# A stick-breaking attention trunk on one core: the hold on the next weights moved from ScalarE's tile to GpSimd's, and one block of w per head pair multiplied by VectorE

## The chip, the core and the metric

The kernel runs on one core of a Trainium2 chip. The core has TensorE (PE in the profile; PEld is its weight load), VectorE (DVE), ScalarE (ACT), GpSimd (POOL) and SyncE (SP), which here issues all the DMA transfers of the program's own. The five engines run their own instruction streams, each in the order in which the program was built, and meet through semaphores. The metric is the device time of one execution in microseconds (us); a kernel's time is the median over its runs.

## The reference, cut to what matters

One layer: half a SwiGLU block, stick-breaking attention, half a SwiGLU block, each behind an RMS norm, on 1024 rows of 1024 columns. The change touches the attention alone (16 heads of 64):

```python
qkv = xn @ w_qkv                       # q, k normalised per head
z = q . k / sqrt(64)                   # per head, blocks of 128 queries
A[t,s] = sigmoid(z[t,s]) * prod_{s<j<t} (1 - sigmoid(z[t,j]))   # s < t
o = A @ v ;  x = x + o @ w_o
```

## The kernel before, in words

Every matrix product is made of three passes: an operand is split into a high part (a copy in fp32r, made by ScalarE) and a low part (the rest, a subtraction made by GpSimd or VectorE), and high x high, low x high and high x low are summed in PSUM. The rows are stored in reverse order, so that the product over j becomes a scan that runs forward.

The attention works on eight **pairs of heads**, one after the other. While the scores of pair p are worked on, TensorE also computes q, k and v of pair p+1 ("fills", `qkv`, nine or six matmuls at a time, 128x384, on the banks bq), and the weights of pair p+2 are loaded and split (`weights_of`). A pair has four parts a to d (head 1 or 0, rows of the lower or upper half).

- **Scores** (`scores`): for each block `(tb, kb)` TensorE writes z into a bank bz (L817), ScalarE makes two sigmoids of it (L821: into w, and in place in bz), VectorE runs the product scan over bz into the tile om (L823), and GpSimd multiplies w by om (L830), after a memset of one column (L828) where a row block begins. For the upper half of the rows om lies in the same buffer as w and the profile calls both w.
- **Values** (`values`): TensorE transposes w by blocks into a bank bt (L852), ScalarE copies that into th (L179), VectorE subtracts th from the bank into tl (L180), and TensorE multiplies th and tl with v into the bank bo (L870). There are two tiles each of th and tl and two banks bt.
- **Weights of pair p+2** (`weights_of`): four steps k = 0, 2, 4, 6 per pair. A step loads `raw_qkv` by two DMAs (L701; 192 KB each), makes the high part wqh of it (L707, ScalarE, 128x768) and the low part wql (L710, GpSimd, two of 128x384). Steps 0 and 2 fill one pair of tiles wqh and wql, steps 4 and 6 another; I call them the **first tile** and the **second tile**. `raw_qkv` has two buffers, so the load of a step can begin only when the copy and both subtractions of the step two before it are done.
- **The hold**: without more, the copy could run as soon as its load has landed. Before L707 a step therefore lets GpSimd write a value that is thrown away, made from a place of qk that is computed late in pair p+1's fills (L706): into one column of wqh. ScalarE's copy overwrites that column and so has to wait for GpSimd's write.
- **Order**: the code gives every piece of work a place in time (`PARTS`, `FILLS`, `LOADS`, in us of a plan), sorts by it, and the framework's scheduler then settles when the program is built in which order each engine issues its instructions. Nothing is reordered on the chip: an instruction that waits holds up all that stand behind it on its engine.

The names in the profile: q_s, kh_s, kl_s are the splits of q and k (L779 on ScalarE, L780 on VectorE) from banks bz that hold transposed qk (L775); sq, qk and vst (L739, L740, L743) are ScalarE's three readings of a finished fill; o (L875, L876) is a finished output, which is split into w tiles (L179, L180) and stored (o_keep).

Of the kernel before, what the change touches and what calls it, by code (L numbers as in the profile page):

```python
# [13 lines left out]
ALU = mybir.AluOpType  # L14
# [3 lines left out]
P = 128  # L18
# [85 lines left out]
def macaron_kernel(ctx, tc, x, g1, w1_in, w1_out, gm, w_qkv, gq, gk, w_o, g2, w2_in, w2_out, out):  # L104
    nc = tc.nc
    act, dve, pool_e, pe, sp = nc.scalar, nc.vector, nc.gpsimd, nc.tensor, nc.sync
# [42 lines left out]
    def bank(tag):  # L149
        p, used = psum[-1]  # L150
        if tag not in IN_TURN:
            return p.tile([P, NHALF], F32, name=tag, bufs=BANKS[tag])
        i = used[tag] = (used.get(tag, -1) + 1) % BANKS[tag]
        return p.tile([P, NHALF], F32, name=f"{tag}{i}", bufs=1)
# [434 lines left out]
    with pools(*RAWS) as pr:  # L589
# [41 lines left out]
        with banks("ps2"), pools(*SECOND) as pl:  # L631
            lay_banks()
            gain_m = load_gain(pn, gm)
            half = pn["xs"].tile([P, 4, 2], F32, name="half", bufs=1)
# [41 lines left out]
    with ExitStack() as stack:  # L676
# [9 lines left out]
        def weights_of(p, state, behind=None):  # L686

            wh, wl = state["wq"] = {}, {}

            def step(n, k):
                if k % 4 == 0:
                    wq = pl[f"wq{(2 * p + k // 4) % 4}"]
                    state["h"], state["l"] = (wq.tile([P, 4, 3 * P], F32R, name=f"wq{n}", bufs=1) for n in "hl")
                h_, l_ = state["h"], state["l"]
                raw = pl["raw_qkv"].tile([P, 2, 3, P], F32, name="raw_qkv")
                src = w_qkv[k * P : (k + 2) * P, :].rearrange("(k p) (a c) -> p k a c", p=P, a=3)
                for i in range(2):  # L700
                    sp.dma_start(raw[:, i], src[:, i, :, p * P : (p + 1) * P])  # L701
                ks = slice(k % 4, k % 4 + 2)
                raw = raw.rearrange("p k a c -> p k (a c)")
                if behind:
                    there = behind[n]()
                    pool_e.tensor_tensor(h_[:, k % 4, 0:1], there, there, op=ALU.mult)  # L706
                act.activation(h_[:, ks], raw, AF.Copy)  # L707
                for i in range(2):
                    k_ = k % 4 + i
                    pool_e.tensor_tensor(l_[:, k_, :], raw[:, i, :], h_[:, k_, :].bitcast(F32), op=ALU.subtract)  # L710
                    wh[k + i], wl[k + i] = h_[:, k % 4 + i, :], l_[:, k % 4 + i, :]

            return [partial(step, i // 2, k) for i, k in enumerate((4, 6, 0, 2) if p == 0 else (0, 2, 4, 6))]
# [83 lines left out]
        def scores(state, hd, half):  # L797

            w = state["w", hd, half] = {}

            def step(tb, kb):
                L = T - tb * P
                if kb == half:
                    t = pl["w"].tile([P, T - tb % 4 * P], F32, name=f"w{hd}{tb % 4}", bufs=1)

                    om = t[:, L : 2 * L] if half else pl["om"].tile([P, T], F32, name="om")
                    state["om"], w[tb] = om, t[:, :L]
                om, wt = state["om"], w[tb]
                q = state["q", hd, half][:, (tb % 4) * P : (tb % 4 + 1) * P]
                s0 = max(tb * P, kb * NHALF)  # L810
                n = (kb + 1) * NHALF - s0
                c0 = s0 - tb * P
                off = P if n == P else 0
                z = bank("bz")
                keys = slice(s0 - off - kb * NHALF, NHALF)
                for i in range(2):
                    pe.matmul(z[:, : off + n], q, state["k", hd, kb][i][:, keys], start=i == 0, stop=i == 1)  # L817

                z = z[:, off : off + n]
                for to, sign in ((wt[:, c0 : c0 + n], 0), (z, 1)):  # L820
                    act.activation(to, z, AF.Sigmoid, scale=state["f", half][:, sign, tb % 4, hd : hd + 1])  # L821
                least = first[:, P : P + 1].to_broadcast([P, n]) if c0 else first[:, :n]
                dve.tensor_tensor_scan(  # L823
                    om[:, c0 : c0 + n], z, least, initial=om[:, c0 - 1 : c0] if c0 else 0.0,
                    op0=ALU.mult, op1=ALU.max,
                )
                if c0 == 0:
                    pool_e.memset(wt[:, 0:1], 0.0)  # L828
                c1 = max(c0, 1)
                pool_e.tensor_tensor(wt[:, c1 : c0 + n], wt[:, c1 : c0 + n], om[:, c1 - 1 : c0 + n - 1], op=ALU.mult)  # L830

            return [partial(step, tb, kb) for tb in range(half * 4, half * 4 + 4) for kb in range(half, 2)]

        def values(state, p, hd, half):
# [263 lines left out]
```

## Time and profile before

| What | us |
|---|---|
| Time before, median of 3 runs (lowest, highest) | 1968.99 (1968.15, 1970.13) |
| The profiled execution's own time | 1967.96 |
| Its span in the trace | 1966.2 |
| One steady pair, from one transpose L852 to the same one of the next pair (814.91 to 881.74) | 66.83 |
| TensorE busy in that pair | 64.89 |
| VectorE, ScalarE, GpSimd busy in that pair | 52.29, 51.29, 38.34 |

The trace has the eight pairs between some 700 us and 1240 us from the span's start; feed-forward blocks lie before and behind. Five steady pairs follow each other at the same distance, so a place in one pair is found again 66.8 us later. In a line of the timeline the first number is the start in us, the second the duration, then engine, line, operation, tiles and shapes; square brackets give how long the engine sat idle just before, and which instruction ended that idle time.

### The profile page before, as it was taken

Reading aid. Unit: us, or ns where it says so; the run is one execution under the profiler, and the core shown is the slowest. Engines: PE = TensorE matmul, PEld = TensorE weight load, DVE = VectorE, ACT = ScalarE, POOL = GpSimd, SP = SyncE. Lnnn points to the kernel's source line nnn. Section 1 sums busy time; section 2 is a strip of 40 time slices with the busy share of each in tenths; the row PEclk is TensorE's granted clock in tenths of the full one; section 3 lists DMA queues with packets and bytes.
Section 4 is the critical chain, followed back from the end, with each engine's and each line's share of the span. In section 5 each row is a group of like instructions: output and inputs, shape, how many; then the busy total and the mean of one; then the engine's idle time right before and its main releaser. Section 6 shows DMA issues by size and latency. Waiting matters only on the chain.

```text
span 1966.2 us, 27322 instructions
## 1 busy us (share of the span) xinstructions
PE 1917.2 (98%) x9656; PEld 1641.7 (83%) x9656; DVE 1248.8 (64%) x1823; ACT 983.4 (50%) x1802; POOL 1086.9 (55%) x957
## 2 busy tenths in 40 slices
PE   7999999999999899999999999999999999999999
PEld 7978888888888798898889897789888888888887
DVE  7855545536767667877787778474645644547644
ACT  6533433443335467777777776344343343343332
POOL 3667666656445445555655645113666666755454
PEclk9999999999999999999999999999999999999999
DMA  5223323238996311111111234411332332359984
GB/s 209 86 93 122 106 88 120 95 123 287 355 321 222 105 33 44 38 39 44 36 37 42 66 103 164 166 60 54 118 102 100 121 102 86 124 195 350 317 274 148
DMA packets 168504, 260.25 MB, mean 132 GB/s; under 512 B 11568, under 2 KB 81200, under 8 KB 168368
## 3 DMA queue, kind: packets, MB, share of 16 engines
q1 hardware_dynamic: 168368, 258.52, 38.3%
q8 instruction: 75, 1.23, 0.3%
q14 instruction: 61, 0.50, 0.1%
HBM read 198.18 MB, written 60.29 MB: 131 GB/s over the span
## 4 chain that ended last, share of the span: by engine, by line
PE 79%; DVE 9%; POOL 4%; ACT 4%; issue 3%; DMA 1%; SPq 0%; ACTq 0%; DVEq 0%; POOLq 0%
PE ka L271 6%; PE ka L272 6%; PE ka L273 6%; PE kc L273 4%; PE kc L272 4%; PE kc L271 4%; PE kb L272 4%; PE kb L273 4%; PE kb L271 4%; PE bq L271 3%; PE bq L272 3%; PE bq L273 3%; PE ma L271 3%; PE ma L272 3%; PE ma L273 3%
## 5 line engine op out<-in xcount | busy, mean ns | idle before, releaser
L180 POOL TENSOR_TENSOR rp<-raw,rp 128x1024 fp32r<-128x1024 f32 x84 | 205.8, 2453 | 189.7 <-ACT rp L179 174.5
L180 POOL TENSOR_TENSOR u<-sf,u 128x512 fp32r<-128x512 f32 x160 | 225.9, 1413 | 152.3 <-ACT u L179 148.4
L180 POOL TENSOR_TENSOR u<-raw,u 128x512 fp32r<-128x512 f32 x136 | 195.8, 1445 | 173.4 <-ACT u L179 172.4
L830 POOL TENSOR_TENSOR w<-w,om 128x512 f32<-128x512 f32 (+4 forms) x128 | 142.4, 1115 | 120.0 <-DVE om L823 93.6
L179 ACT ACTIVATE u<-sf 128x512 fp32r<-128x512 f32 x160 | 100.7, 630 | 215.3 <-PE kb L272 86.8
L390 DVE TENSOR_TENSOR h<-h 128x512 f32<-128x512 f32 x110 | 135.3, 1235 | 88.6 <-POOL h L494 87.9
L271 PE MATMUL bq<-wqh,xh 128*128 128x384 f32 x512 | 174.6, 341 | 2.1 <-DVE vst L744 2.1
L179 ACT ACTIVATE rp<-rh 128x1024 fp32r<-128x1024 f32 (+1 forms) x78 | 76.5, 984 | 198.4 <-issue 65.4
L273 PE MATMUL bq<-wqh,xl 128*128 128x384 f32 x512 | 172.2, 336 | 0.0
L272 PE MATMUL bq<-wql,xh 128*128 128x384 f32 x512 | 172.1, 336 | 0.0
L271 PE MATMUL ka<-xh,u 128*128 128x512 f32 (+1 forms) x448 | 162.2, 362 | 1.9 <-ACT s L442 1.4
L179 ACT ACTIVATE u<-raw 128x512 fp32r<-128x512 f32 x136 | 85.0, 632 | 154.9 <-PE ka L272 101.3
L272 PE MATMUL ka<-xl,u 128*128 128x512 f32 (+1 forms) x448 | 161.9, 361 | 0.0
L273 PE MATMUL ka<-xh,u 128*128 128x512 f32 (+1 forms) x448 | 161.6, 361 | 0.0
L515 DVE TENSOR_TENSOR raw<-raw 128x1024 f32<-128x1024 f32 (+1 forms) x60 | 86.4, 1445 | 96.4 <-DMA raw<-w_out 76.4
L273 PE MATMUL ma<-rp 128*128 128x512 f32 x352 | 137.6, 391 | 3.6 <-DVE rp L180 3.6
L271 PE MATMUL ma<-rp 128*128 128x512 f32 x352 | 137.9, 392 | 0.1
L272 PE MATMUL ma<-rp 128*128 128x512 f32 x352 | 137.6, 391 | 0.0
L821 ACT ACTIVATE w<-bz,f 128x512 f32<-128x512 f32 (+1 forms) x192 | 112.8, 587 | 46.2 <-PE bz L817 40.6
L494 POOL TENSOR_TENSOR h<-h,g 128x512 f32<-128x512 f32 x80 | 112.5, 1406 | 32.7 <-DVE h L446 32.7
L419 DVE TENSOR_TENSOR sf<-raw 128x512 f32<-128x512 f32 x80 | 80.2, 1003 | 78.0 <-POOL u L180 78.0
L180 DVE TENSOR_TENSOR rp<-rh,rp 128x1024 fp32r<-128x1024 f32 (+1 forms) x70 | 110.0, 1590 | 19.2 <-ACT rp L179 16.7
(253 smaller groups left out, 5550.1 us busy)
## 6 DMA issues: line engine op xcount, KB each, us to landing
raw<-w_out SPq DMA_DIRECT2D x120, 512.0 KB, 5.7
raw<-w_in SPq DMA_DIRECT2D x88, 512.0 KB, 3.5
k<-h SPq DMA_DIRECT2D x154, 256.0 KB, 2.1
rh<-k SPq DMA_DIRECT2D x64, 512.0 KB, 6.0
raw_qkv<-w_qkv SPq DMA_DIRECT2D x64, 192.0 KB, 2.9
x_keep<-x SPq DMA_DIRECT2D x32, 256.0 KB, 2.9
x<-x_keep SPq DMA_DIRECT2D x32, 256.0 KB, 5.0
raw<-w_out SPq DMA_DIRECT2D x24, 256.0 KB, 4.2
```

The costliest lines, as they stand in the source:

```text
L179: act.activation(hi, raw, AF.Copy)
L180: (engine or dve).tensor_tensor(lo, raw, hi.bitcast(F32), op=ALU.subtract)
L271: pe.matmul(dst, ah, bh, start=start and i == 0, stop=False, skip_group_check=onto)
L272: pe.matmul(dst, ah, bl, start=False, stop=False, skip_group_check=onto)
L273: pe.matmul(dst, al, bh, start=False, stop=stop and i == n - 1, skip_group_check=onto)
L390: dve.tensor_tensor(src, hb[of[0]], hb[of[1]], op=getattr(ALU, of[2]))
L419: dve.tensor_tensor(f[n], x, y, op=op)
L494: pool_e.tensor_tensor(h, h, gs[k], op=ALU.mult)
L515: dve.tensor_tensor(w[0], w[0], w[1], op=getattr(ALU, W_OF[m][2]))
L821: act.activation(to, z, AF.Sigmoid, scale=state["f", half][:, sign, tb % 4, hd : hd + 1])
L830: pool_e.tensor_tensor(wt[:, c1 : c0 + n], wt[:, c1 : c0 + n], om[:, c1 - 1 : c0 + n - 1], op=ALU.mult)
```

## The change

Two edits. The value that GpSimd writes to hold a step is now written into wql, the low part, in the first column of both row groups that the step fills (two elements), so that only GpSimd's own subtractions come after it; ScalarE's copy no longer has anything of the hold to wait for. And of head 0, lower rows, the last block of the last row group (`tb` 3, `kb` 1: 128x512) is multiplied by om on VectorE, no longer on GpSimd: one block in each of the eight pairs.

```diff
                 if behind:
-                    there = behind[n]()
-                    pool_e.tensor_tensor(h_[:, k % 4, 0:1], there, there, op=ALU.mult)
+                    there = behind[n]().to_broadcast([P, 2])
+                    pool_e.tensor_tensor(l_[:, ks, 0], there, there, op=ALU.mult)
                 act.activation(h_[:, ks], raw, AF.Copy)
...
                 c1 = max(c0, 1)
-                pool_e.tensor_tensor(wt[:, c1 : c0 + n], wt[:, c1 : c0 + n], om[:, c1 - 1 : c0 + n - 1], op=ALU.mult)
+
+                engine = dve if (hd, half, tb, kb) == (0, 0, 3, 1) else pool_e
+                engine.tensor_tensor(wt[:, c1 : c0 + n], wt[:, c1 : c0 + n], om[:, c1 - 1 : c0 + n - 1], op=ALU.mult)
```

Behind L830 the line numbers of the changed kernel are two higher (L852 is L854). The order of the instructions moves as follows; numbers in names are the program's tile numbers, the same in both kernels. The first place is ScalarE at 889 to 900 us of the trace before, where TensorE has just got past the fills of pair p+1; wqh_8906 is a first tile, wqh_9124 the second tile of the same weights. Before:

```order
L821 ACTIVATE bz_8875<-bz_8875,f0_8367 128x256
L707 ACTIVATE wqh_8906<-raw_qkv_8908 128x768
L739 ACTIVATE sq_8889<-bq_8825 128x256
L740 ACTIVATE qk0_8823<-bq_8825 128x256
L743 ACTIVATE vst_8421<-bq_8825 128x2x64
L179 ACTIVATE th_8902<-bt_8897 128x512
L821 ACTIVATE w12_8873<-bz_8915,f0_8367 128x512
L821 ACTIVATE bz_8915<-bz_8915,f0_8367 128x512
L707 ACTIVATE wqh_8906<-raw_qkv_8943 128x768
L779 ACTIVATE q_s1_8937<-bz_8932,gq_sb_6221 64x512
L179 ACTIVATE th_8956<-bt_8952 128x384
```

And now, on the same engine at the same place:

```order
L179 ACTIVATE th_8902<-bt_8897 128x512
L821 ACTIVATE w12_8873<-bz_8915,f0_8367 128x512
L821 ACTIVATE bz_8915<-bz_8915,f0_8367 128x512
L779 ACTIVATE q_s1_8937<-bz_8932,gq_sb_6221 64x512
L707 ACTIVATE wqh_9124<-raw_qkv_9126 128x768
L179 ACTIVATE th_8956<-bt_8952 128x384
L779 ACTIVATE q_s1_8940<-bz_8932,gq_sb_6221 64x512
L821 ACTIVATE w13_8960<-bz_8962,f0_8367 128x128
L821 ACTIVATE bz_8962<-bz_8962,f0_8367 128x128
L707 ACTIVATE wqh_9124<-raw_qkv_9162 128x768
L779 ACTIVATE kh_s1_8979<-bz_8981,gk_sb_6223 128x512
```

The copies of the first tile are gone from here, and those of the second tile stand here instead, one of them ahead of th_8956. The loads raw_qkv_9126 and raw_qkv_9162 go into the buffers of raw_qkv_8908 and raw_qkv_8943. Their own copies have moved to the second place, ScalarE at 840 to 850 us, about 50 us earlier, where the copies of the second tile of the weights before them (wqh_8281) stood. Before:

```order
L179 ACTIVATE th_8256<-bt_8251 128x512
L707 ACTIVATE wqh_8281<-raw_qkv_8283 128x768
L707 ACTIVATE wqh_8281<-raw_qkv_8319 128x768
L779 ACTIVATE kh_s1_8270<-bz_8272,gk_sb_6223 128x512
L179 ACTIVATE th_8295<-bt_8290 128x512
L821 ACTIVATE w02_8310<-bz_8311,f1_7945 128x256
```

Now:

```order
L179 ACTIVATE th_8256<-bt_8251 128x512
L779 ACTIVATE kh_s1_8270<-bz_8272,gk_sb_6223 128x512
L179 ACTIVATE th_8295<-bt_8290 128x512
L707 ACTIVATE wqh_8906<-raw_qkv_8908 128x768
L707 ACTIVATE wqh_8906<-raw_qkv_8943 128x768
L821 ACTIVATE w02_8310<-bz_8311,f1_7945 128x256
L821 ACTIVATE bz_8311<-bz_8311,f1_7945 128x256
L179 ACTIVATE th_8331<-bt_8326 128x512
```

So at both places the copies are now those of loads that come one tile later. The third place is VectorE at 877 to 884 us, where the multiplication comes in (w03_8693 is the tile, om_8694 its product):

```order
 L823 SCALAR_TENSOR_TENSOR om_8694<-bz_8725,om_8694,first_6511 128x512
 L180 TENSOR_TENSOR w13_8720<-o1_8501,w12_8719 128x512
+L832 TENSOR_TENSOR w03_8693<-w03_8693,om_8694 128x512
 L823 SCALAR_TENSOR_TENSOR om_8733<-bz_8734,first_6511 128x512
 L823 SCALAR_TENSOR_TENSOR om_8733<-bz_8751,om_8733,first_6511 128x512
```

VectorE does it behind the split of o and ahead of the next two scans. On GpSimd the subtractions L710 keep their places but for one block of w or two: those of a second tile now stand directly behind their hold, ahead of the multiplication of 128x383 that they followed. TensorE's order in a pair and SyncE's are as before, but for two matmuls of a fill that now stand among the last four of bo.

## Prediction

> **What bounds the kernel now.** I read the page first (busy shares), then the busy times of one steady pair, then the table of waits, then the timeline of each engine through one pair. The page's first line and the stretch of one steady pair (its length, then busy us and instructions of PE, PEld, DVE, ACT and POOL, the granted clock, and the DMA's share and GB/s):
>
> ```profile
> PE 1917.2 (98%) x9656; PEld 1641.7 (83%) x9656; DVE 1248.8 (64%) x1823; ACT 983.4 (50%) x1802; POOL 1086.9 (55%) x957
> 814.91:881.74 66.83, 64.89 (x388) 59.28 (x389) 52.29 (x100) 51.29 (x114) 38.34 (x58) 1.00 0.13 40
> ACT wqh L707 <- POOL wqh L706: 12.3, 6, 2.1
> ```
>
> TensorE sets the time: in a pair it stands still for 66.83 - 64.89 = 1.94 us. So nothing another engine saves is worth more than that a pair, while what makes TensorE wait longer is open above. The third line (who waited for whom, us in total, times, longest) is the wait that the first edit removes: ScalarE stood 2.06 us at the hold, six times. Here is its place, which I call A: ScalarE, then TensorE.
>
> ```profile
> 892.24 0.85 ACT L707 ACTIVATE wqh<-raw_qkv 128x768 fp32r<-128x768 f32 x1 [2.06 <-POOL wqh L706]
> 895.29 0.88 ACT L707 ACTIVATE wqh<-raw_qkv 128x768 fp32r<-128x768 f32 x1
> 896.02 0.69 ACT L779 ACTIVATE q_s<-bz,gq_sb 64x512 fp32r<-64x512 f32 x1
> 896.59 0.49 ACT L179 ACTIVATE th<-bt 128x384 fp32r<-128x384 f32 x1
> 899.12 0.60 ACT L179 ACTIVATE th<-bt 128x512 fp32r<-128x512 f32 x1
> 893.08 0.60 PE L775 MATMUL bz<-ident,qk 128*128 128x128 f32 x4
> 894.33 0.51 PE L870 MATMUL bo<-th,vst 128*128 128x512 f32 x1 [0.65 <-ACT th L179]
> 895.06 0.50 PE L870 MATMUL bo<-tl,vst 128*128 128x512 f32 x1 [0.22 <-DVE tl L180]
> 897.91 0.42 PE L870 MATMUL bo<-th,vst 128*128 128x384 f32 x1
> 898.17 0.41 PE L870 MATMUL bo<-tl,vst 128*128 128x384 f32 x1
> 900.37 0.28 PE L870 MATMUL bo<-th,vst 128*128 128x256 f32 x1
> ```
>
> ScalarE's 2.06 us at the hold made th late, and TensorE waited 0.65 us for th and 0.22 us for tl: 0.87 us of the pair's 1.94.
>
> **The first edit: what the hold now leaves open.** ScalarE's copy waits for its load instead, and at place A the copies now in the queue are those of the second tile, whose loads go into the buffers of the first. A buffer is free when GpSimd has done both subtractions. GpSimd and SyncE at A:
>
> ```profile
> 892.90 0.73 POOL L830 TENSOR_TENSOR w<-w,om 128x255 f32<-128x255 f32 x1
> 893.59 1.96 POOL L710 TENSOR_TENSOR wql<-raw_qkv,wqh 128x384 fp32r<-128x384 f32 x2
> 895.58 20.25 SPq L701 DMA_DIRECT2D raw_qkv<-w_qkv  x8
> ```
>
> Two subtractions ended at 893.59 + 1.96 = 895.55, and the next load was issued at 895.58: it does wait for them, and SyncE had nothing else to do (its order is unchanged, and behind these loads only the stores of o queue). In the changed order the two stand ahead of that multiplication (0.73 us), so the buffer is free at 894.82 in the same frame. The hold itself cannot release GpSimd sooner: it waits for GpSimd's own work on qk just before.
>
> How long from a free buffer to the copy is measured in the ramp, where ScalarE came to two such copies early (GpSimd's four subtractions, SyncE's loads, ScalarE's copies):
>
> ```profile
> 685.79 4.38 POOL L710 TENSOR_TENSOR wql<-raw_qkv,wqh 128x384 fp32r<-128x384 f32 x4 [0.52 <-ACT wqh L707]
> 688.26 9.87 SPq L701 DMA_DIRECT2D raw_qkv<-w_qkv  x8
> 691.94 0.84 ACT L707 ACTIVATE wqh<-raw_qkv 128x768 fp32r<-128x768 f32 x1 [4.79 <-DMA raw_qkv<-w_qkv]
> 694.01 0.84 ACT L707 ACTIVATE wqh<-raw_qkv 128x768 fp32r<-128x768 f32 x1 [1.22 <-DMA raw_qkv<-w_qkv]
> ```
>
> Issue at 688.26, copy at 691.94: 3.68 us. The last subtraction ended at 685.79 + 4.38 = 690.17, the second copy began at 694.01: 3.84 us. ScalarE waited 4.79 and 1.22 us there. I take 3.7. [...]
>
> At A the first copy so starts at 894.82 + 3.7 = 898.5. ScalarE itself is there early: without the hold and the two old copies it is through q_s by about 894.4, and stands some 4 us. The copy frees ScalarE 0.73 us later (895.29 to 896.02), so the 384-wide th runs from 899.25 to 899.75 and tl is ready at some 900.35. TensorE, which took that th at 897.91 and that tl at 898.17, starts them at 899.8 and 900.4: 2.2 us later than before, although its two old waits are gone. Its next th was wanted 900.37 - 898.17 = 2.2 us after that, at 902.6. But the third and fourth subtractions, now behind the multiplication, end at 894.82 + 0.73 + 1.96 = 897.5, the second copy starts at 901.2, and 0.73 us later kh_s and then th follow (about 0.6 us each), ready at 903.15: 0.55 us late, and tl costs some 0.15 us more. TensorE leaves A **2.9 us** later than before. It happens six times. In the ramp the same edit moves two holds; ScalarE waits for loads there already, and I take nothing (1.2 us either way, the wait at 694.01).
>
> Place B, 50 us earlier in the pair, has the first tile's copies now, and the same chain: hold, subtractions of the second tile, loads, copies. GpSimd, ScalarE, TensorE before:
>
> ```profile
> 840.35 0.35 POOL L706 TENSOR_TENSOR wqh<-qk 128x1 fp32r<-128x1 f32 x2
> 844.20 0.65 ACT L179 ACTIVATE th<-bt 128x512 fp32r<-128x512 f32 x1
> 846.45 0.47 ACT L821 ACTIVATE w<-bz,f 128x256 f32<-128x256 f32 x1 [1.60 <-PE bz L817]
> 847.18 0.60 ACT L179 ACTIVATE th<-bt 128x512 fp32r<-128x512 f32 x1
> 848.47 0.48 PE L870 MATMUL bo<-th,vst 128*128 128x512 f32 x1
> 848.79 0.40 PE L870 MATMUL bo<-tl,vst 128*128 128x512 f32 x1
> ```
>
> The hold ends at 840.70; four subtractions of 0.98 us follow at once and free the buffers at 842.66 and 844.62. The copies so start at 846.36 and 848.3, where ScalarE is ready at 844.8. The sigmoid of 846.45 moves to 849.05 and the th of 847.18 to 849.8, done at 850.4; its tl is done some 0.7 us later. TensorE takes them at 850.4 and 851.2, not at 848.47 and 848.79: **2.4 us**, five times (the last pairs load nothing more).
>
> **The second edit.** VectorE multiplies a block of 128x512, which no row of before shows on it. Nearest rows: its subtraction of two tiles of this size in this stage, 0.70 us, and its sums of two in the feed-forward blocks, 1.235 us. Then the place:
>
> ```profile
> L180 DVE TENSOR_TENSOR w<-o,w 128x512 fp32r<-128x512 f32 x14 | 9.8, 699 | 0.0
> L390 DVE TENSOR_TENSOR h<-h 128x512 f32<-128x512 f32 x110 | 135.3, 1235 | 88.6 <-POOL h L494 87.9
> 880.47 1.21 DVE L823 TENSOR_TENSOR_SCAN om<-bz,first 128x512 f32<-128x512 f32 x1
> 883.50 0.68 DVE L180 TENSOR_TENSOR tl<-bt,th 128x512 fp32r<-128x512 f32 x1
> 881.74 0.76 PE L852 MATMUL bt<-ident,w 128*128 128x128 f32 x5 [0.64 <-POOL w L828]
> 884.32 0.41 PE L870 MATMUL bo<-tl,vst 128*128 128x512 f32 x1
> ```
>
> The first is the same stage and the instruction just before it, so I take 0.70. The block takes the scan's place at 880.47 and is done at 881.17, where TensorE had waited until 881.74: that gives back up to 0.54 us. But VectorE runs without a gap there: the scan starts 0.6 us late, a wait of its own swallows 0.2, and the tl of 883.50 ends at 884.6. TensorE took it at 884.32, with 0.14 us to spare. So the gain is spent 3 us on, and 0.3 us is lost: **+0.3**, eight times; bounds are -0.54 (VectorE's lead holds) and +0.85 (1.235 us).
>
> **What the waits do to the clock.** TensorE's waits grow to 3 us, and the trace has such gaps (three rows of TensorE, then stretches behind them; the third figure from the right is the granted clock):
>
> ```profile
> 650.26 0.50 PE L273 MATMUL ma<-rp 128*128 128x512 f32 x1 [3.65 <-DVE rp L180]
> 1129.94 0.39 PE L817 MATMUL bz<-kh_s,q_s 128*128 128x256 f32 x1 [2.05 <-DVE w L823]
> 1189.62 0.33 PE L852 MATMUL bt<-ident,w 128*128 128x128 f32 x1 [1.84 <-POOL w L828]
> 650.00:660.00 10.00, 9.74 (x36) 7.89 (x37) 1.94 (x3) 3.92 (x6) 8.66 (x7) 0.83 0.30 89
> 1130.00:1132.00 2.00, 2.00 (x12) 1.74 (x12) 1.82 (x4) 1.98 (x6) 1.55 (x4) 1.00 0.68 250
> 1190.00:1200.00 10.00, 10.00 (x52) 8.29 (x51) 8.06 (x18) 5.93 (x12) 5.11 (x8) 0.83 0.80 263
> ```
>
> Behind 3.65 us, and behind 1.84 us, ten us ran at 0.83: 1.7 us lost. Behind 2.05 us the clock stayed. A's gap is 3.0 us: without its old waits TensorE is there at 897.91 - 0.87 - 2 x 0.1 (restarts, 0.51 and 0.50 against 0.40) = 896.8, and th comes at 899.8. So I count a dip each time, at 1.0 us net, since a slower TensorE no longer waits the 0.55 + 0.15 us at the second copy: 6 x 1.0 = 6.0. B's gaps are 1.9 and 0.5 us: a dip every other time, 2.5 x 1.7 = 4.2.
>
> **The sum**, in us: A 6 x 2.9 = 17.4; B 5 x 2.4 = 12.0; VectorE's block 8 x 0.3 = 2.4; clock 6.0 + 4.2 = 10.2; less 2.0 for small waits of TensorE as the 0.22 above, which behind 11 longer ones no longer arise (0.2 each). That is +40.0 on the profiled execution's 1967.96 (span 1966.2), so 2008.0; the median lies 1.03 above that execution: **2009.0**.
>
> **Rivals.**
>
> *The loads come in time (faster).* Then the hold was all that kept ScalarE: 6 x 0.87 = 5.2 us are won at A, and 8 x 0.64 = 5.1 at VectorE's block if its lead holds: 1958.7. For it speak the 12.3 us in the waits. Against it: TensorE wants the 384-wide th at 896.8, so the copy would have to start 0.73 + 0.49 us sooner, by 895.6, which is 0.8 us after the buffer is free; two rows say 3.68 and 3.84. Chance 0.07.
>
> *The waits fall into slack.* If th and tl were ahead of TensorE by as much as the copies are late, gains and losses would cancel near 1969. But TensorE already waits for them at A. Chance 0.05.
>
> *No dips.* The clock stays at 1.00, as behind 2.05 us: 40.0 - 10.2 = +29.8, so 1998.8. [...] The trace speaks against it with the dip behind 1.84 us, and for it with the 2.05. Chance 0.22.
>
> *A dip behind every wait of A and B.* Clock 6.0 + 5 x 1.7 = 14.5: 2013.3. Chance 0.16.
>
> **How the numbers follow.** The forecast itself has 0.50. A measurement of this kernel tells about 0.2% (4 us) from no change. All but the first two rivals are slower by more than that: 0.88; faster 0.07; within 0.2% 0.05. Low end of the range: no dips, VectorE's block at -0.54 (8 x 0.84 = 6.7 less), the loads 0.3 us quicker at the eleven places (3.3): 1998.8 - 10.0 = 1988.8, taken as 1988. High end: all dips and the block at 0.85 (8 x 0.55 = 4.4): 2017.7, taken as 2018. Outside lie the two rivals of 0.12 and a little of the rest.
>
> **What would show it.** Right: ScalarE's waits for the hold are gone from the table, and in their place stand waits of L707 for the load of raw_qkv of 3 to 4 us at A and of 1 to 2 us at B, eleven places in all; TensorE's idle time before bo (L872) at the 384-wide th grows from nothing to about 3 us; a steady pair takes 72 to 74 us; the granted clock in a pair falls under 1.00. Wrong in its main step, if L707 waits for no load in the steady pairs; wrong in the second edit, if a pair's wait at the transposes of w is gone and no wait for tl stands 3 us behind it; wrong in the clock, if pairs with 3 us gaps show 1.00.

## The result, and the profile after

The changed kernel takes **2012.95 us** (median of 4 runs, 2011.69 to 2018.98); the kernel before, run beside it, 1969.26 (4 runs, 1968.15 to 1970.13). The ratio is 1.0224, 95% interval 1.0207 to 1.0242: slower, by 43.7 us, where 2009.0 was forecast (1988 to 2018).

The page's first line of the changed kernel, beside the first one shown of before:

```profile
PE 1938.0 (96%) x9656; PEld 1660.0 (82%) x9656; DVE 1259.4 (62%) x1831; ACT 988.5 (49%) x1802; POOL 1078.4 (53%) x949
```

TensorE runs the same 9656 instructions and is busy 20.8 us longer with them, so part of the loss is a slower TensorE; the rest is standing still. A stretch in which the clock is granted at half I call a **dip** (0.50 from 789.00 to 792.41 us, for one). Stretches of the changed kernel, from the 384-wide th of place A to the same one of the next pair, then pieces behind A and B (length, busy us of PE, PEld, DVE, ACT and POOL, granted clock, DMA share, GB/s):

```profile
766.56:842.02 75.46, 68.42 (x389) 62.28 (x389) 52.80 (x102) 52.14 (x113) 36.82 (x57) 0.95 0.12 36
917.80:991.58 73.78, 66.88 (x389) 60.66 (x389) 52.79 (x102) 52.11 (x113) 36.82 (x57) 0.97 0.12 38
766.00:768.00 2.00, 1.29 (x6) 0.81 (x6) 1.31 (x2) 1.95 (x6) 0.10 (x1) 1.00 0.53 155
768.00:772.00 4.00, 3.88 (x15) 3.75 (x15) 2.95 (x5) 3.62 (x8) 0.46 (x1) 0.57 0.00 0
772.00:776.00 4.00, 4.00 (x26) 3.88 (x26) 1.98 (x5) 1.83 (x3) 1.39 (x2) 1.00 0.00 0
788.00:792.00 4.00, 3.68 (x12) 3.12 (x13) 2.85 (x9) 2.48 (x8) 1.28 (x3) 0.63 0.00 0
```

A pair was 66.83 us with TensorE idle for 1.94 of them. The first pair here is 75.46 with 75.46 - 68.42 = 7.04 idle and 68.42 - 64.89 = 3.5 us more busy at a clock of 0.95: two dips, one behind each place. The third pair shows one dip only and is 73.78. Who waited for whom, attention stage (us in total, times, longest):

```profile
ACT wqh L707 <- DMA raw_qkv<-w_qkv: 37.1, 15, 4.4
PE bo L872 <- ACT th L179: 27.6, 11, 3.4
PE bo L872 <- DVE tl L180: 8.9, 17, 0.9
PE bt L854 <- POOL w L828: 1.8, 1, 1.8
```

The row of before in which L707 waits for GpSimd's hold is gone. In its place L707 waits for its load, and TensorE waits eleven times for th. The place itself, in the timeline of the changed kernel: GpSimd and SyncE at A, ScalarE and TensorE at A, then at B, then VectorE's block and the tl behind it, and a row near the end of the program:

```profile
835.89 1.01 POOL L710 TENSOR_TENSOR wql<-raw_qkv,wqh 128x384 fp32r<-128x384 f32 x1
836.92 3.82 SPq L701 DMA_DIRECT2D raw_qkv<-w_qkv  x4
835.74 0.68 ACT L779 ACTIVATE q_s<-bz,gq_sb 64x512 fp32r<-64x512 f32 x1 [0.77 <-PE bz L775]
840.74 0.84 ACT L707 ACTIVATE wqh<-raw_qkv 128x768 fp32r<-128x768 f32 x1 [4.32 <-DMA raw_qkv<-w_qkv]
841.49 0.47 ACT L179 ACTIVATE th<-bt 128x384 fp32r<-128x384 f32 x1
842.02 0.45 PE L872 MATMUL bo<-th,vst 128*128 128x384 f32 x1 [3.27 <-ACT th L179]
843.21 0.84 ACT L707 ACTIVATE wqh<-raw_qkv 128x768 fp32r<-128x768 f32 x1
783.68 0.85 ACT L707 ACTIVATE wqh<-raw_qkv 128x768 fp32r<-128x768 f32 x1 [1.41 <-DMA raw_qkv<-w_qkv]
785.91 0.84 ACT L707 ACTIVATE wqh<-raw_qkv 128x768 fp32r<-128x768 f32 x1 [1.39 <-DMA raw_qkv<-w_qkv]
788.02 0.49 PE L872 MATMUL bo<-th,vst 128*128 128x512 f32 x1 [1.82 <-ACT th L179]
788.81 0.65 PE L872 MATMUL bo<-tl,vst 128*128 128x512 f32 x1 [0.30 <-DVE tl L180]
821.88 0.69 DVE L832 TENSOR_TENSOR w<-w,om 128x512 f32<-128x512 f32 x1
826.25 0.50 PE L872 MATMUL bo<-tl,vst 128*128 128x512 f32 x1 [0.88 <-DVE tl L180]
1992.97 0.50 PE L273 MATMUL ma<-rp 128*128 128x512 f32 x1 [3.57 <-DVE rp L180]
```

Read A from the top: the second subtraction ends at 836.90, the load is issued at 836.92, the copy can begin at 840.74. ScalarE had been free since 836.42 and stood 4.32 us; th, next in its queue, follows at 841.49; TensorE, which had been waiting for it, starts at 842.02 after 3.27 us. The second copy (843.21) waits for nothing. At B both copies wait 1.4 us, and TensorE 1.82 and 0.30.

The last row lies in the feed-forward block, where the change touches nothing. Such a wait, of 3.3 to 3.6 us, stands there in three of the ten profiled executions of this study: with both edits, with the second alone, and with neither (the run below with no hold on GpSimd). This execution took 2018.98, 6 us over the median, and the wait makes most of that. The pairs are not affected.

### The profile page after: what moved, and what is told of

The parts are those of the page before. It is cut to its first block, busy times and chain, and to the rows that moved or that the text cites. A ratio compares the mean times of both kernels' runs of the same rounds, so it can differ in the third digit from the quotient of the medians.

```text
span 2017.2 us, 27373 instructions
## 1 busy us (share of the span) xinstructions
PE 1938.0 (96%) x9656; PEld 1660.0 (82%) x9656; DVE 1259.4 (62%) x1831; ACT 988.5 (49%) x1802; POOL 1078.4 (53%) x949
## 5 line engine op out<-in xcount | busy, mean ns | idle before, releaser
L832 POOL TENSOR_TENSOR w<-w,om 128x512 f32<-128x512 f32 (+4 forms) x120 | 129.5, 1082 | 125.7 <-DVE om L823 99.7
L271 PE MATMUL bq<-wqh,xh 128*128 128x384 f32 x512 | 179.3, 350 | 1.3 <-DVE vst L744 1.3
L515 DVE TENSOR_TENSOR raw<-raw 128x1024 f32<-128x1024 f32 (+1 forms) x60 | 93.3, 1558 | 93.0 <-DMA raw<-w_out 85.0
L180 DVE TENSOR_TENSOR tl<-bt,th 128x512 fp32r<-128x512 f32 (+1 forms) x160 | 104.9, 656 | 51.2 <-ACT th L179 49.5
```

What stands on the lines that cost most here:

```text
L180: (engine or dve).tensor_tensor(lo, raw, hi.bitcast(F32), op=ALU.subtract)
L271: pe.matmul(dst, ah, bh, start=start and i == 0, stop=False, skip_group_check=onto)
L515: dve.tensor_tensor(w[0], w[0], w[1], op=getattr(ALU, W_OF[m][2]))
L832: engine.tensor_tensor(wt[:, c1 : c0 + n], wt[:, c1 : c0 + n], om[:, c1 - 1 : c0 + n - 1], op=ALU.mult)
```

## The experiments

My theory: the copies now stand in ScalarE's queue right behind loads that cannot begin before GpSimd's hold and its subtractions, and TensorE pays for that in waits for th and in clock dips behind them. The rivals: VectorE's block, or the hold in wql itself, carries a good part. Times are medians beside the kernel before on the same chip (1969.43 with the first four, 1968.75 with the others).

**The first edit alone.** The block goes back to GpSimd:

```diff
-                engine = dve if (hd, half, tb, kb) == (0, 0, 3, 1) else pool_e
+                engine = pool_e
```

> The first edit alone: the hold is written into wql, and the block of w stays with GpSimd. My theory (copies that stand in ScalarE's queue right behind a load that cannot begin before the hold, and a clock dip of 1.7 us behind nearly every wait of TensorE that this makes): 2011, between 2006 and 2015, with L707 waiting 4 us at place A and 1.4 us at place B as in the changed kernel, steady pairs of some 75 us; the pair's wait at the transposes of w (0.64) is there again and the wait for tl (0.87) is gone. Rival, VectorE's block carries a good part of the loss: under 2000.

Measured 2015.29 (2013.65 to 2018.42), just above the expected range, ratio 1.0234 (1.0216 to 1.0251). Its waits in the attention stage:

```profile
ACT wqh L707 <- DMA raw_qkv<-w_qkv: 34.1, 16, 4.5
PE bo L872 <- ACT th L179: 27.6, 11, 3.4
```

These are the rows of the whole change: 11 waits for th, 27.6 us. The first edit makes the loss alone. The interval overlaps that of the whole change, so the second edit makes no difference beside the first that can be told.

**The second edit alone.**

```diff
-                pool_e.tensor_tensor(wt[:, c1 : c0 + n], wt[:, c1 : c0 + n], om[:, c1 - 1 : c0 + n - 1], op=ALU.mult)
+                engine = dve if (hd, half, tb, kb) == (0, 0, 3, 1) else pool_e
+                engine.tensor_tensor(wt[:, c1 : c0 + n], wt[:, c1 : c0 + n], om[:, c1 - 1 : c0 + n - 1], op=ALU.mult)
```

> The second edit alone: the block of 128x512 on VectorE, the hold as before. My theory, from the changed kernel's own rows (a wait of 0.64 us gone, one of 0.87 us new, eight times): +2 us, so 1971, between 1966 and 1975. Rival, the block carries a good part of the 44 us: over 1980. Rival, VectorE's lead holds once ScalarE is not late: 5 us less than before, 1964.

Measured 1973.41 (11 runs, 1971.26 to 1979.11), ratio 1.0019 (1.0007 to 1.0031): +4.0 us, where +2 was expected. VectorE and TensorE in this kernel, at the place of the block:

```profile
881.69 0.69 DVE L831 TENSOR_TENSOR w<-w,om 128x512 f32<-128x512 f32 x1
882.29 1.22 DVE L823 TENSOR_TENSOR_SCAN om<-bz,first 128x512 f32<-128x512 f32 x1
881.85 1.35 PE L853 MATMUL bt<-ident,w 128*128 128x128 f32 x8
886.06 0.50 PE L871 MATMUL bo<-tl,vst 128*128 128x512 f32 x1 [0.87 <-DVE tl L180]
```

The eight transposes run through without the wait of 0.64, and the tl behind them costs 0.87. So the time that VectorE gains by being early at the transposes is lost again here, where ScalarE is in time as well.

**One tile alone.** The hold moves to wql for steps 4 and 6 only:

```diff
-                    pool_e.tensor_tensor(h_[:, k % 4, 0:1], there, there, op=ALU.mult)
+                    if n == 1:
+                        there = there.to_broadcast([P, 2])
+                        pool_e.tensor_tensor(l_[:, ks, 0], there, there, op=ALU.mult)
+                    else:
+                        pool_e.tensor_tensor(h_[:, k % 4, 0:1], there, there, op=ALU.mult)
```

> The hold is moved to wql for the second tile alone (steps 4 and 6); the first tile keeps it in wqh, and the block stays with GpSimd. The orders of TensorE, VectorE and SyncE are those of before; on ScalarE the copies of the second tile now stand at place A behind those of the first, one ahead of the second q_s, one behind o. My theory: the first of them stands 1.8 us before its load has landed (buffer free at 895.55, copy at 899.3, in the queue at 897.55), so the next 512-wide th is ready at 902.1, where TensorE wants it at 900.4: a new wait of some 1.8 us, six times, and most of them with a dip of 1.7 us: +20, so 1989, between 1979 and 2000. Rival, there is slack for so short a wait: 1969. Rival, only the loss of the hold in the first tile counts: 1969 or less.

Measured 1986.45 (1986.21 to 1987.37), ratio 1.0086 (1.0071 to 1.0102). ScalarE and TensorE at A in this kernel (its line numbers from L707 on are four higher than those of before):

```profile
975.56 0.85 ACT L711 ACTIVATE wqh<-raw_qkv 128x768 fp32r<-128x768 f32 x1 [1.93 <-DMA raw_qkv<-w_qkv]
978.37 0.39 PE L874 MATMUL bo<-th,vst 128*128 128x256 f32 x1 [1.74 <-ACT th L179]
979.34 0.39 PE L874 MATMUL bo<-tl,vst 128*128 128x256 f32 x1 [0.58 <-DVE tl L180]
```

The copy waits 1.93 us where 1.8 was worked out, TensorE 1.74 for th. With TensorE's, VectorE's and SyncE's order as before, one copy that stands behind its load costs 17 us in six pairs, three of them with a dip. There is no slack for 1.8 us.

**The gaps filled.** The changed kernel, with matmuls of zeros ahead of the late th (zeros: the zero part of the tile `first`, made fp32r):

```diff
                     vv = state["v"][:, sb, 2 * hd : 2 * hd + 2, :].rearrange("p a b -> p (a b)")
+                    for _ in range({(0, 0, 2): 16 if p < NP - 2 else 0, (1, 0, 3): 9 if p < NP - 3 else 0}.get((hd, half, sb), 0)):
+                        pe.matmul(ot[:, : 3 * P], vv, zeros[:, P:], start=False, stop=False)
```

> The changed kernel, with matmuls of zeros (128x384) in front of the two th for which TensorE waits in a pair: 16 at place A (2.8 us), 9 at place B (1.6 us). They add zeros to bo, so nothing else is computed; the orders of ScalarE, GpSimd and SyncE stay but for a few rows. They need nothing that is late, so they fill the idle time and th comes no later. My theory (the clock falls because TensorE stood still): the granted clock in a pair is 1.00 again and 10 to 11 dips of 1.7 us go: 17 to 19 us less than the changed kernel, 1995, between 1990 and 2001. Rival, the dips have another cause, or come anyway: 2013. Rival, the matmuls cost their own time: over 2020.

Measured 2006.53 (2003.82 to 2009.10), ratio 1.0187 (1.0170 to 1.0205): 6.4 us under the changed kernel, not 17, and outside the expected range. A pair of this kernel, and TensorE at A and, in the last row, at the th of B:

```profile
840.95:916.25 75.30, 70.91 (x413) 63.37 (x413) 53.31 (x102) 51.99 (x113) 36.86 (x57) 1.00 0.13 39
763.13 3.03 PE L871 MATMUL bo<-first,vst 128*128 128x384 f32 x16
766.41 0.44 PE L874 MATMUL bo<-th,vst 128*128 128x384 f32 x1 [0.25 <-ACT th L179]
770.01 0.39 PE L874 MATMUL bo<-th,vst 128*128 128x256 f32 x1 [0.24 <-ACT th L179]
770.91 0.39 PE L874 MATMUL bo<-tl,vst 128*128 128x256 f32 x1 [0.51 <-DVE tl L180]
787.58 0.50 PE L874 MATMUL bo<-th,vst 128*128 128x512 f32 x1 [0.18 <-ACT th L179]
```

The clock is 1.00 in the pair: the dips do come from TensorE standing still. But my price for them was wrong. At full speed TensorE comes too early to what the second copy holds up: it waits 0.51 us for tl at all six places A (and here 0.24 for th), which it does not in the changed kernel. A dip at A stands mostly in place of that wait. The fill also let a few of TensorE's rows at B change places (a tl of 384 now ahead of both score matmuls that it stood between), and two waits for tl are new behind them, of 0.23 and 0.30 us in the first pair. So what a dip at B costs is better read from other runs, below.

**The hold in wql, the copies in their old places.** The first edit alone, plus a write of ScalarE's own:

```diff
+                if early:
+                    act.activation(h_[:, k % 4, 0:1], early[n](), AF.Copy)
                 act.activation(h_[:, ks], raw, AF.Copy)
...
-            weights_of(p + 2, states[p + 2], held)
+            weights_of(p + 2, states[p + 2], held, (lambda s=nxt: s["qk", 0][:, 0, 0, 0:1], held[1]))
```

> The first edit stays (GpSimd's hold in wql, the block with GpSimd), and ScalarE's copies are kept in their old places by a write of ScalarE's own into wqh, made from a column of qk that ScalarE itself wrote just before, so that it waits for nobody. TensorE's, VectorE's and SyncE's orders are those of before. My theory (the loss is wholly that the copies stand right behind late loads): L707 waits for no load in the steady pairs, the 0.87 us of TensorE at place A are gone as well, and the time is 1969 - 6 x 0.87 = 1964, between 1961 and 1970. Rival, the hold in wql itself costs (GpSimd's two columns, the subtractions that follow it at once): over 1975.

Measured **1959.93** (1957.96 to 1963.56), just under the expected range, ratio 0.9959 (0.9944 to 0.9974). A pair, and ScalarE at A (L709 is the copy, L708 the write):

```profile
827.89:893.21 65.32, 64.31 (x391) 59.27 (x390) 52.24 (x101) 51.67 (x116) 38.13 (x58) 1.00 0.13 41
887.38 0.29 ACT L745 ACTIVATE vst<-bq 128x128 fp32r<-128x128 f32 x1
887.53 0.31 ACT L708 ACTIVATE wqh<-qk 128x1 fp32r<-128x1 f32 x2
887.78 0.85 ACT L709 ACTIVATE wqh<-raw_qkv 128x768 fp32r<-128x768 f32 x1
888.53 0.58 ACT L179 ACTIVATE th<-bt 128x512 fp32r<-128x512 f32 x1
```

No row waits. (The first copy stands behind ScalarE's three readings of the fill, sq, qk and vst, and no longer ahead of them; the rest of the order here is that of before.) The hold stands where the change put it, and the kernel is 8.8 us faster than before: what costs 44 us in the change is the place of the copies in ScalarE's queue, nothing else of the first edit.

**No hold on GpSimd.** The hold of before replaced by that write of ScalarE's:

```diff
-                    there = behind[n]()
-                    pool_e.tensor_tensor(h_[:, k % 4, 0:1], there, there, op=ALU.mult)
+                    act.activation(h_[:, k % 4, 0:1], behind[n](), AF.Copy)
...
-                held = (lambda s=nxt: s["qk", 1][:, 0, 4, 0:1], lambda s=nxt: s["qk", 0][:, 2, 0, 0:1])
+                held = (lambda s=nxt: s["qk", 0][:, 0, 0, 0:1], lambda s=nxt: s["qk", 0][:, 2, 0, 0:1])
```

> As the run with the copies kept in place, but GpSimd writes no hold at all: only ScalarE's own write into wqh holds a step. My theory: the subtractions follow the copies by data anyway, so this is the same time, 1964, between 1961 and 1970. Rival, GpSimd's hold costs the path something of its own: 3 us or more between the two.

Measured 1960.70 (1958.35 to 1963.37), ratio 0.9958 (0.9944 to 0.9972). This differs from the run just above by 0.8 us, within the spread of both: GpSimd's hold has no price of its own that can be told.

**The hold earlier.** The changed kernel with other values to wait for:

```diff
-                held = (lambda s=nxt: s["qk", 1][:, 0, 4, 0:1], lambda s=nxt: s["qk", 0][:, 2, 0, 0:1])
+                held = (lambda s=nxt: s["qk", 1][:, 2, 0, 0:1], lambda s=nxt: s["qk", 0][:, 0, 0, 0:1])
```

> The changed kernel with both holds made from values that are there earlier (qk of row group 2 of the first half, and of row group 0 of the second, column 0): GpSimd writes the first hold some 17 us before place A, the second at place A. The scheduler moves ScalarE's copies of place A some 8 us ahead, the others stay. My theory: what costs is the distance from the hold to the copy; a buffer is free some 9 us before the copy here, a load takes 3.7, so L707 waits for no load and TensorE for no th at A and B: 1969 - 5 + 4 (the second edit as measured) = 1968, between 1960 and 1980, granted clock 1.00 in a pair. Rival, the scheduler always sets the copies right behind the loads, so they wait wherever the hold is: over 1995. Rival, GpSimd's four subtractions now stand ahead of products that TensorE waits for: up to 8 x 2 us more, 1985.

Measured 1965.46 (12 runs, 1963.63 to 1974.17), ratio 0.9989 (0.9977 to 1.0001): the loss is gone, the copies wait for no load in the steady pairs. One late wait per pair is new beside the tl of the second edit: TensorE's transposes of w for VectorE's block, 0.65 us.

**The same with the block back on GpSimd.**

> The same with the block of 128x512 back on GpSimd. My theory: GpSimd is 4 us later with the products behind its subtractions, its block as well, so TensorE's wait at the transposes of w (0.64) grows by 0 to 1 us eight times; against it the second edit's 4 us are saved: 1966, between 1958 and 1976. Rival, the block on VectorE is what makes room for early subtractions: slower than the run with the block on VectorE by over 5 us.

The edit is that of the first run on top of the seventh. Measured **1959.93** (1958.38 to 1961.49), ratio 0.9952 (0.9940 to 0.9965). GpSimd's subtractions, ScalarE's copies and TensorE at the transposes of w:

```profile
874.17 1.99 POOL L710 TENSOR_TENSOR wql<-raw_qkv,wqh 128x384 fp32r<-128x384 f32 x2
876.15 1.98 POOL L710 TENSOR_TENSOR wql<-raw_qkv,wqh 128x384 fp32r<-128x384 f32 x2
882.80 1.57 ACT L707 ACTIVATE wqh<-raw_qkv 128x768 fp32r<-128x768 f32 x2
880.28 0.76 PE L854 MATMUL bt<-ident,w 128*128 128x128 f32 x5 [1.32 <-POOL w L828]
```

The last subtraction ends at 878.13, the copies begin at 882.80, 4.7 us later: enough for a load of 3.8. GpSimd's products do come later, TensorE waits 1.32 instead of 0.64, and still this is 5.5 us faster than with the block on VectorE. Beside the first run (2015.29) the code differs only in the values that the holds wait for: 55 us.

## Why the prediction was right, and where its sizes were off

**The path of the loss: right.** The hold's waits are gone, L707 waits for raw_qkv at eleven places, 4.15 to 4.42 us at A (3 to 4 forecast, about 4 in the working) and 1.0 to 1.5 at B (one idle time of 1.71 there ends with TensorE's bz). From issue to copy the load takes 840.74 - 836.92 = 3.82 us; 3.7 was used. (That SyncE's row is 3.82 long too is chance: it spans the issues of two loads, at 836.92 and 839.54.) TensorE's gap at the 384-wide th was forecast at 3.0 and is 3.08 to 3.36.

**The sum, piece by piece.** Three marks of TensorE per pair give the pieces: the 384-wide th of A, the 512-wide th of B, the tl behind the block. First pair after: 766.56, 788.02, 826.25, 842.02; before (rows of the prediction): 848.47, 884.32, 897.91, and 66.87 earlier than the last for the first.

| Piece | before | after, mean of five pairs | lost | forecast |
|---|---|---|---|---|
| A to B (second copy, a dip at A, first wait of B) | 17.43 | 21.33 | 3.9 | 0.7 + 1.0 + 1.9 = 3.6 |
| B to the tl (rest of B, a dip, the block) | 35.85 | 38.05 | 2.2 | 0.5 + 0.85 + 0.3 = 1.65 |
| tl to A (gap of 3 us less the old waits) | 13.59 | 15.72 | 2.1 | 2.2 |

That is 8.2 us a pair where these terms make 7.45. A pair was stated to take 72 to 74 us and takes 73.8 to 75.8, four of the five over that. Five pairs with 0.8 more make 4.0, and the 2.0 that was taken off did not come either (below). So the attention stage of the profiled execution, from TensorE's wait for vst in the ramp to its wait of 1.84 us for w near the end (695.94 to 1189.62 before, 696.33 to 1235.78 after), is 45.8 us longer where 40.0 was forecast; the medians came out 4.0 over the forecast.

**The terms that were mis-sized.** The second edit: +0.3 was taken from "TensorE took it at 884.32, with 0.14 us to spare"; the wait for tl is 0.87 against the 0.64 that goes, and alone the edit costs 4.0 us, where 2.4 stood, inside its bounds. The chance of a dip at B: "a dip every other time"; it came in four of five. The 2.0 us taken off for small waits that would "no longer arise": of TensorE's two of 0.15 and 0.28 us some 11 to 16 us behind the th of B, the second stands in all five pairs after, the first in two, and in a third it has grown to 0.52, so nothing came of it there. The gain at the transposes that the working gave up was rightly given up.

**The clock.** "1.0 us net" at A was the right thought and still too much: with the gap filled, A to B is 787.58 - 766.41 = 21.17 us in the first pair and 20.99 on average over five, with a dip 21.33, so 0.3 net. A dip at B is not covered: the one pair without it took 73.78, the other four 75.43 on average, 1.65 apart. The one-tile run says the same with more pairs (from the late th to that of the next pair): 71.10 and 70.85 with a dip, 69.32, 69.53 and 69.16 without, 1.64 apart. Six times 0.3 and four times 1.65 make 8.4, where 10.2 was in the sum: right by two errors that cancel, too dear at A and too rare at B. The rival "a dip behind every wait", 2013.3, names the time better, but it priced A's dips at what they do not cost. That the total was close is in part luck, then: with the clock 1.8 us cheaper than forecast, the other terms were some 7.6 us too small in the profiled execution: 1.6 for the block, the 2.0, and some 4 that no run here shows apart (what TensorE's restarts cost, at the end of this document, would be of that size).

**The other rivals.** "The loads come in time", 1958.7, is not what the change does; but when the loads are made to come in time, by the old places or by an earlier hold, the time is 1959.93 twice. "Slack" falls with the one-tile run. "No dips", 1998.8: with the dips taken away the time is 2006.5; what is over I put down to the dearer block, to TensorE's restarts (below) and to the rows that the fill moved at B, which was not tried apart.

Open in part: why the first edit alone is not faster than both, when the second alone costs 4.0. Its profile has four long dips of 6.8 us at A (below) where the changed kernel's has one. From A to B it takes 21.80 us on average, 0.47 more than the changed kernel, and from B to the next A 0.40 less, so in this execution the long dips use up what the block saves. Whether its other executions had as many is not on record.

## What to carry to other kernels

A wait that is moved off one engine may have been what kept that engine's other work in place: before removing a hold, ask where the scheduler will put the instruction that it held, and compare the distance to its data with the measured time of the load. Here a buffer's release, its refill and its next use lay within one load time of 3.8 us, and the load was on the path although the DMA engines were busy for 0.12 of the pair. Moving the releases ahead, by some 17 us for place A and 12 for place B, was worth 55 us. Keeping the copies in their places by a write of ScalarE's own was worth as much, with GpSimd's hold or without it. And price a clock dip by what is late behind it: here it cost 1.65 us at place B and in the one-tile run, and 0.3 at place A, where TensorE would else have waited for what the second copy held up.

## What the runs showed of the hardware

The clock fell behind gaps much shorter than the dip is long, and not behind all of them. In the one-tile run TensorE stood 1.41 us and dipped, for some 3.4 us, and stood 1.76 us and did not (TensorE's row and the stretch behind it, twice):

```profile
1118.38 0.39 PE L874 MATMUL bo<-th,vst 128*128 128x256 f32 x1 [1.41 <-ACT th L179]
1119.88:1123.38 3.50, 3.50 (x12) 3.38 (x12) 1.99 (x4) 1.65 (x4) 1.28 (x1) 0.51 0.02 5
908.84 0.39 PE L874 MATMUL bo<-th,vst 128*128 128x256 f32 x1 [1.76 <-ACT th L179]
908.84:915.84 7.00, 6.41 (x39) 6.06 (x40) 5.15 (x8) 5.26 (x11) 2.15 (x3) 1.00 0.02 7
```

In the changed kernel's trace the dips begin whole multiples of 3.41 us from one another (768.52, 789.00, 843.62, 864.10, 918.71, 990.39 and 1014.28 follow each other by 6, 16, 6, 16, 21 and 7 of them), so there the clock changed on a grid of steps of 3.41 us. TensorE's idle time in the step of the grid just ahead told more than the length of one gap. Those steps for the two gaps above (the second gap lies across two):

```profile
1116.51:1119.92 3.41, 1.41 (x8) 0.90 (x7) 2.53 (x4) 3.38 (x8) 0.00 (x0) 1.00 0.40 115
904.88:908.29 3.41, 2.20 (x13) 1.78 (x12) 0.75 (x2) 2.20 (x4) 1.59 (x4) 1.00 0.26 72
908.29:911.71 3.42, 2.28 (x13) 2.09 (x14) 3.19 (x7) 3.40 (x9) 0.39 (x1) 1.00 0.19 56
```

TensorE was idle for 3.41 - 1.41 = 2.00 us of the first, and for 1.21 and 1.14 us of the others. In the traces of the changed kernel and of the kernel before, between 700 and 1240 us, a dip began behind all 7 full-clock steps with 1.85 us idle or more (2.66 at most), behind 6 of 10 with 1.55 to 1.84, and behind none with less (idle by the profile, which models the ends of matmuls).

Over the changed kernel, the first edit alone and the one-tile run, a dip stood at each of 12 gaps of 2.99 us or more at A, and behind 12 of 16 gaps of th between 1.4 and 2.0. Most began 0.7 to 2.3 us behind the end of the wait and lasted 3.4 us. Five of those at A, one in the changed kernel and four with the first edit alone, began 0.5 to 1.2 us before the wait ended and lasted two steps, 6.8 us. One of them, from 914.67 to 921.50 (first edit alone; the stretch shown begins at the end of the wait):

```profile
915.17 0.69 PE L872 MATMUL bo<-th,vst 128*128 128x384 f32 x1 [3.43 <-ACT th L179]
915.17:921.17 6.00, 6.00 (x20) 5.42 (x21) 4.54 (x7) 5.07 (x11) 0.89 (x3) 0.50 0.05 15
```

A wait seems to cost TensorE more than its idle time. The run with the copies in their old places has two waits fewer a pair than before (0.65 and 0.22 idle), and TensorE's busy time in a pair fell as well, from 64.89 to 64.31 at a clock of 1.00: about 0.3 us for each restart, by my estimate from these two runs. Six pairs of 0.87 + 0.58 make 8.7 us, which would account for the 8.8 that it won, where the idle time alone said 5.2. The price is not the same at every wait: in the second edit alone, where a wait of 0.87 stands in place of one of 0.64, TensorE's busy time rose to 65.25 and 65.16 us in two pairs. No run here shows what the restarts behind the waits of the change itself cost.
